# Filter spectra stored twice in DRAM, the last filter unit dealt out over two stages, the last convolution block loaded ahead

## The chip, the cores and the metric

The kernel runs on one core of one Trainium2 chip. The metric is device time in microseconds (us): the median of three runs. A core has TensorE (PE, matrix products into PSUM), VectorE (DVE), ScalarE (ACT), GpSimd (POOL) and SyncE (SP). Sixteen DMA engines move data between DRAM and on-chip memory (SBUF, 128 partitions); here SyncE's queue issues nearly all transfers. Each queue is worked off in order: an issue that waits holds up everything behind it.

## The reference

One layer on 2048 positions of 1024 channels, in float32:

```
p   = rmsnorm(x) @ w_in                      # 512 Fourier channels, 3 x 512 Hyena
y_f = rmsnorm(Re(FFT2 of the Fourier channels in 8 groups of 64))
x1, x2, v = split(short_conv(p[:, 512:]))    # three taps
k   = filters(...)                           # 2 orders x 512 channels x 4096 taps, unit norm
z   = x1 * (long_conv(v, k[0]) + d[0] * v)   # FFT over 4096 points
z   = x2 * (long_conv(z, k[1]) + d[1] * z)
y_h = rmsnorm(z)
x   = x + concat(y_f, y_h) @ w_out
out = rmsnorm_final(x + relu(rmsnorm(x) @ w_fc1)**2 @ w_fc2)
```

The filters come from a small sine network on positions, times a decay, and are normalised; `long_d` holds the d.

## The kernel before

Products that need it are made of three passes over split high and low parts. In order of time: the projection (`project`, until 410 us), with a generator `tables` run between its steps that loads tables; the Fourier mix (`fourier`) together with the first filter units, until about 475; the other filter units until 628; the long convolutions (`hyena`) until about 855; the output projection and the two MLP products until the end.

**Filters** (`filters`, lines 496 to 652). Eight units, one for each order n (0, 1) and each tile ct of 128 channels. `generate(q)`, q = 0 to 7, makes an eighth of a filter: four products into PSUM (L529), times the decay read from DRAM (`dec`, two buffers, one for two q), split into `kh` and `kl`, squares summed on GpSimd. `normalise` turns the sum into a scale and folds `long_d` in; `skip` puts it on the first tap. `stage1(c)` is the first step of a 4096-point transform, turned by VectorE (L443, tile `Gk`); `stage2(q)` is the second, with the table `f2` as the stationary operand (L597), copied to `ks` by ScalarE (L600) and stored by SyncE for two q together (L602) into the scratch `kd` ("spec" in the profile). A spectrum lies there as 128 rows: 64 frequencies of the real part, then 64 of the imaginary part.

While unit i goes through its sixteen steps (eight of `stage1`, eight of `stage2`), unit i + 2 is generated between them, by the list GENERATE; unit 7 is generated within unit 5's steps. Within unit 6's second half unit 7's `stage1` runs too (LAST). When tile `zz` is free (it held a unit's filter), v is read back into it (L648) and scaled by the product of the two filters' scales (`scale`, L582). A planner sets the order on each queue from program order and its own cost model, and moves instructions ahead where an engine would be idle.

**Convolutions** (`hyena`, from L655). Eight blocks, one for each (n, ct). `first(c)` and `second(q)` transform the input (L691, L698), with the same `f2`; `spectrum(q)` reads an eighth of the spectrum; y = pz * ks[:, 0] + (swapped, signed pz) * ks[:, 1], the first product on VectorE, the second on GpSimd, the sum on either (L704 to L706). `inverse(q)` (L714), `turn(c)` and `gate(q)` go back and multiply with the gate, read as `xg` (L670). Steps of up to four blocks are interleaved; the inverse is three steps behind (LAG). For the multiplication every partition needs both the real and the imaginary part, so `spectrum` reads the rows twice, by two transfers of 64 partitions into a tile with four buffers:

```
ks = hp.tile([P, 2, 4, 128], F32, tag="ks", name="ks", bufs=4)
src = kd[...][:, 4 * q : 4 * q + 4, :].rearrange("(s p) f c -> p s f c", s=2)
for hf in (slice(0, 64), slice(64, 128)):
    nc.sync.dma_start(ks[hf], src)
```

After the last block's steps come its gates and inverse, `Out.ahead` (the Fourier rows of the first two tokens' tiles are read, normalised, turned and multiplied with the first half of `w_out`), and `Out.weights`, which reads `w_out` and splits it into the tiles G and V that the blocks used.

Of the kernel before, what the change touches and what calls it, by code (L numbers as in the profile page):

```python
# [10 lines left out]
F32 = mybir.dt.float32  # L11
# [15 lines left out]
def _tables():  # L27
# [3 lines left out]
    T = {}  # L31
# [52 lines left out]
    A2[:, 0, 0] *= 0.5  # L84
    T["f2"] = F2.reshape(128, 32, 128).astype(f32)
# [49 lines left out]
def hybrid_block(ctx: ExitStack, tc: tile.TileContext, A, out):  # L135
# [9 lines left out]
    kd = [[scratch(f"spec{i}{n}", [P, 32, 128]) for n in range(2)] for i in range(4)]  # L145
# [350 lines left out]
    def filters(ctx, fp, gp, zp, zzs, norms, emb, wo, e1k, f2):  # L496
# [6 lines left out]
        rows = fp.tile([8, 128], F32, tag="dk8", name="dk8")  # L503
        for n in range(2):
            nc.sync.dma_start(rows[4 * n : 4 * n + 4, :], A["long_d"].rearrange("a (c n) j -> n (a c) j", n=2)[n])
        p = pa("plongd")
        nc.tensor.transpose(p[:, 0:8], rows, ident[0:8, 0:8])
        nc.scalar.copy(longd, p[:, 0:8])

        class Unit:  # L510
# [83 lines left out]
            def stage2(self, q):  # L594
# [6 lines left out]
                if q % 2:  # L601
                    nc.sync.dma_start(kd[self.ct][self.n][:, 4 * q - 4 : 4 * q + 4, :], self.ks)  # L602
# [12 lines left out]
        GENERATE = [(3, 5, 7, 7, 9, 11, 13, 15)] * 5 + [(7, 7, 8, 9, 10, 11, 12, 13)]  # L615

        LAST = ((), (), (), (), (), (0, 1, 2), (3, 4, 5), (6, 7))
        for i, u in enumerate(units):
            new = units[i + 1] if i < 7 else None

            def generate(step):
                for q in range(8 if i < 6 else 0):
                    if GENERATE[i][q] == step:
                        units[i + 2].generate(q)

            for c in range(8 if new else 0):
                u.stage1(c)
                if i == 0 and c == 6:
                    new.normalise()
                generate(c)  # L630
            for q in range(8):
                u.stage2(q)
                if i == 6:
                    for c in LAST[q]:
                        new.stage1(c)
                if i and new and q == (0 if i == 6 else 1):
                    new.normalise()

                if new and q == (2, 5, 5, 5, 5, 5, 4)[i]:
                    new.skip()  # L640
                generate(8 + q)
                if q % 4 == 0 and i > 4:
                    ct = 2 * i - 11 + q // 4
                    if 0 <= ct < 4:
                        cs = slice(128 * ct, 128 * ct + 128)
                        if ct == 0:
                            zzs.append(zp.tile([P, NT, 512], F32, tag="zz", name="zz"))
                        nc.sync.dma_start(zzs[0][:, :, cs], gd[0][:, :, cs])  # L648
                j = 8 * i + q - 50
                if 0 <= j < 8:  # L650
                    units[j // 2].scale(2 * (j % 2), nc.gpsimd)
                    units[j // 2].scale(2 * (j % 2) + 1, nc.vector)


    def hyena(hp, wp, rp, zz, e1, b1, f2, a2, out_weights, out_ahead):  # L655
# [6 lines left out]
        class Block:  # L662
            def __init__(self, n, ct):
                self.n, self.ct = n, ct
                self.cs = slice(128 * ct, 128 * ct + 128)
                self.y, self.ahead = {}, None
# [5 lines left out]
            def spectrum(self, q):  # L672

                ks = hp.tile([P, 2, 4, 128], F32, tag="ks", name="ks", bufs=4)
                src = kd[self.ct][self.n][:, 4 * q : 4 * q + 4, :].rearrange("(s p) f c -> p s f c", s=2)
                for hf in (slice(0, 64), slice(64, 128)):
                    nc.sync.dma_start(ks[hf], src)
# [16 lines left out]
            def second(self, q):  # L694
                ks = self.ahead if q == 0 and self.ahead else self.spectrum(q)
# [10 lines left out]
                (nc.gpsimd if self is not blocks[7] and q in (0, 1, 2, 3) else nc.vector).tensor_add(y, y, zs)  # L706
# [32 lines left out]
        for i in range(8):  # L739
            cur, old, older, new = (blocks[j] if 0 <= j < 8 else None for j in (i, i - 1, i - 2, i + 1))  # L740
            for q in range(8):
                if new and q == 7:
                    new.ahead = new.spectrum(0)
# [12 lines left out]
                if old and q == 3:  # L756
                    old.load()
                if new:
# [3 lines left out]
        old.load()  # L762
        for q in range(8 - LAG, 8):
            old.inverse(q)
        ahead = out_ahead(hp)
# [667 lines left out]
```

## Time and profile before

| | us |
|---|---|
| median of 3 runs | 2326.68 (2323.57 to 2328.45) |
| the profiled execution | 2326.34 |
| its span in the profile | 2324.5 |
| TensorE busy | 2244.5 (97%) |
| VectorE busy | 1514.7 (65%) |
| ScalarE busy | 1108.8 (48%) |
| GpSimd busy | 827.4 (36%) |

The profile is of one execution. A row of a group gives line, engine, operation, output <- inputs by the program's names, shapes, count, then busy time and the mean of one in ns, then idle time before them and what ended it. "SPq" and "ACTq" are the queues that issue transfers. In a timeline the columns are start, duration, engine, line, operation; in square brackets the idle time before it and its releaser. "PEclk" is the granted TensorE clock (1.00 is full). The rows themselves stand in the prediction.

### The profile page before, as it was taken

How to read it: one execution, taken by the hardware profiler on the slowest of the kernel's cores; microseconds unless marked ns; L12 is line 12 of the kernel's file. 1: busy time of each engine (PE TensorE's matmuls, PEld its weight loads, DVE VectorE, ACT ScalarE, POOL GpSimd, SP SyncE). 2: the span in 40 equal slices, each digit the busy share in tenths (PEclk: the TensorE clock that was granted, in tenths of full speed). 3: DMA queues.
4: the chain of work that ended last, by engine and by line, in shares of the span. 5: the costliest groups of instructions: out<-in, count | busy, mean ns of one | idle time of the engine just before them, and what ended most of it. 6: DMA issues, size and time to landing. Idle time of an engine off the chain costs nothing.

```text
span 2324.5 us, 31068 instructions
## 1 busy us (share of the span) xinstructions
PE 2244.5 (97%) x11025; PEld 1859.5 (80%) x11025; DVE 1514.7 (65%) x2256; ACT 1108.8 (48%) x1842; POOL 827.4 (36%) x625
## 2 busy tenths in 40 slices
PE   7999999899999979998999999999999999999998
PEld 6887788698888758886788877888888888888886
DVE  6999676677677775457544456444366666866667
ACT  6555211465455554445555556555543333533334
POOL 3444332567366532116655556555400000000000
PEclk9999999999999999999999999999999999999999
DMA  7535986557689985667544455444479766866631
GB/s 253 182 136 197 330 303 244 189 194 240 223 194 204 206 235 163 186 177 233 162 152 153 151 205 193 150 150 150 160 283 361 241 191 193 291 207 191 198 119 73
DMA packets 294716, 468.42 MB, mean 202 GB/s; under 512 B 18389, under 2 KB 142623, under 8 KB 290209
## 3 DMA queue, kind: packets, MB, share of 16 engines
q1 hardware_dynamic: 288897, 452.04, 61.3%
q10 hardware_dynamic: 5664, 14.41, 1.8%
q8 instruction: 86, 1.41, 0.3%
q14 instruction: 69, 0.57, 0.1%
HBM read 312.54 MB, written 152.27 MB: 200 GB/s over the span
## 4 chain that ended last, share of the span: by engine, by line
PE 62%; DMA 4%; DVE 4%; ACT 2%; issue 1%; POOL 1%; SPq 1%; POOLq 0%; DVEq 0%; ACTq 0%
PE p1u L189 5%; PE p1u L191 5%; PE p1u L190 5%; PE p2u L191 5%; PE p2u L189 5%; PE p2u L190 5%; PE p2v L189 3%; PE p2v L191 2%; PE p2v L190 2%; PE p1v L189 2%; PE p1v L191 2%; PE p1v L190 2%; DMA ks<-spec 2%; PE po L190 2%; PE po L191 2%; PE po L189 2%
## 5 line engine op out<-in xcount | busy, mean ns | idle before, releaser
L181 ACT CAST qahm<-ra 128x1024 fp32r<-128x1024 f32 x110 | 115.9, 1053 | 345.8 <-PE p2u L190 172.7
L182 DVE TENSOR_TENSOR qalm<-ra,qahm 128x1024 fp32r<-128x1024 f32 x110 | 134.6, 1224 | 154.6 <-ACT qahm L181 151.8
L1208 POOL TENSOR_TENSOR acc<-acc,gfin 128x512 f32<-128x512 f32 x4 | 5.1, 1277 | 633.0 <-DMA out<-acc 625.8
L189 PE MATMUL pu<-wh,xh 128*128 128x512 f32 x512 | 204.2, 400 | 5.8 <-ACT wh L184 4.6
L190 PE MATMUL pu<-wl,xh 128*128 128x512 f32 x512 | 201.1, 393 | 3.3 <-DVE wl L185 3.3
L191 PE MATMUL pu<-wh,xl 128*128 128x512 f32 x512 | 200.9, 393 | 1.7 <-DVE xl L182 1.6
L190 PE MATMUL p2u<-qblm,qahm 128*128 128x512 f32 x504 | 196.2, 389 | 0.5 <-DVE qblm L182 0.5
L189 PE MATMUL p2u<-qbhm,qahm 128*128 128x512 f32 x504 | 196.0, 389 | 0.0
L191 PE MATMUL p2u<-qbhm,qalm 128*128 128x512 f32 x504 | 195.8, 389 | 0.0
L182 DVE TENSOR_TENSOR qblm<-rb,qbhm 128x1024 fp32r<-128x1024 f32 x110 | 134.0, 1218 | 1.9 <-ACT qbhm L181 1.9
L380 POOL TENSOR_TENSOR acc<-acc,cw 128x512 f32<-128x512 f32 x45 | 59.4, 1320 | 201.5 <-DVE acc L357 200.0
L181 ACT CAST ahm<-s 128x512 fp32r<-128x512 f32 x124 | 76.6, 620 | 95.2 <-PE p1v L190 54.6
L182 POOL TENSOR_TENSOR alm<-W,ahm 128x512 fp32r<-128x512 f32 x63 | 85.3, 1354 | 92.9 <-ACT ahm L181 92.9
L189 PEld LDWEIGHTS pu<-wh,xh 128*128 128x128 f32 x512 | 97.1, 190 | 26.4 <-ACT wh L184 5.0
L181 ACT CAST qbhm<-rb 128x1024 fp32r<-128x1024 f32 x110 | 115.4, 1049 | 5.2 <-DMA a1m<-c 3.4
L190 PEld LDWEIGHTS pu<-wl,xh 128*128 128x128 f32 x512 | 97.1, 190 | 24.2 <-DVE wl L185 3.8
L191 PEld LDWEIGHTS pu<-wh,xl 128*128 128x128 f32 x512 | 97.0, 189 | 23.1 <-DVE xl L182 2.5
L190 PEld LDWEIGHTS p2u<-qblm,qahm 128*128 128x128 f32 x504 | 94.6, 188 | 20.6 <-DVE qblm L182 1.0
L189 PEld LDWEIGHTS p2u<-qbhm,qahm 128*128 128x128 f32 x504 | 94.5, 188 | 20.2 <-ACT qbhm L181 0.4
L191 PEld LDWEIGHTS p2u<-qbhm,qalm 128*128 128x128 f32 x504 | 94.6, 188 | 19.8
L189 PE MATMUL p1u<-bm,ahm 128*128 128x512 f32 x252 | 100.2, 398 | 7.2 <-ACT ku L1071 6.3
L181 ACT CAST ahm<-W 128x512 fp32r<-128x512 f32 x94 | 57.6, 615 | 102.5 <-PE p1u L190 96.0
(387 smaller groups left out, 6449.2 us busy)
## 6 DMA issues: line engine op xcount, KB each, us to landing
W<-in_w_fc SPq DMA_DIRECT2D x66, 512.0 KB, 4.6
ks<-spec SPq DMA_DIRECT2D x128, 256.0 KB, 6.6
rb<-td SPq DMA_DIRECT2D x64, 512.0 KB, 4.2
ra<-a1m SPq DMA_DIRECT2D x56, 512.0 KB, 6.8
ra<-a0m SPq DMA_DIRECT2D x54, 512.0 KB, 10.6
rb<-in_w_fc SPq DMA_DIRECT2D x46, 512.0 KB, 4.5
f<-in_w_fc SPq DMA_DIRECT2D x16, 1024.0 KB, 6.8
td<-f SPq DMA_DIRECT2D x16, 1024.0 KB, 5.2
```

Source lines behind the costliest of these rows:

```text
L181: nc.scalar.copy(hi, src)
L182: (eng or nc.vector).tensor_sub(lo, src, hi)
L189: nc.tensor.matmul(o, lhsT=lh, rhs=rh, start=start, stop=False, skip_group_check=more)
L190: nc.tensor.matmul(o, lhsT=lh, rhs=rl, start=False, stop=False, skip_group_check=more)
L191: nc.tensor.matmul(o, lhsT=ll, rhs=rh, start=False, stop=stop, skip_group_check=more)
L380: nc.gpsimd.tensor_add(m1, m1, cw[:, 3, :])
L1208: nc.gpsimd.tensor_mul(acc[i][:, c], acc[i][:, c], gfin[:, c])
```

## The change

The spectrum is written twice and read with one transfer of 128 partitions: the scratch gets the shape (copy, frequency, part, rest), the two parts of a frequency side by side. For that `stage2` gives its rows in the order frequency, part; a second table `f2k` with its columns in that order is loaded in place of `f2`, and while the last unit's `stage2` is done with an eighth after another, `f2` is loaded over it. The store is issued by ScalarE and reads its source twice. The read of `long_d` moves from `filters` to `tables`. Unit 7 is generated in unit 5's second and unit 6's first half; the reads and scalings of `zz` and the steps of the last stage are listed anew. The last block reads its spectra 2 to 7 at its second step, 4 to 7 of them into a tile of the pool `raws`; its gates, the Fourier rows and the first four parts of `w_out` are read within its steps; the work after it is ordered anew, and the tiles that take `w_out` and later the MLP's input alternate between G and V.

```diff
+    T["f2k"] = np.ascontiguousarray(F2.transpose(0, 1, 2, 4, 3)).reshape(128, 32, 128).astype(f32)
...
-    kd = [[scratch(f"spec{i}{n}", [P, 32, 128]) for n in range(2)] for i in range(4)]
+    kd = [[scratch(f"spec{i}{n}", [2, 64, 2, 32 * 128]) for n in range(2)] for i in range(4)]
...
-        rows = fp.tile([8, 128], F32, tag="dk8", name="dk8")
-        for n in range(2):
-            nc.sync.dma_start(rows[4 * n : 4 * n + 4, :], A["long_d"].rearrange("a (c n) j -> n (a c) j", n=2)[n])
...
                 if q % 2:
-                    nc.sync.dma_start(kd[self.ct][self.n][:, 4 * q - 4 : 4 * q + 4, :], self.ks)
+                    dst = kd[self.ct][self.n].rearrange("h p s x -> (p s) h x")[:, :, 512 * q - 512 : 512 * q + 512]
+                    nc.scalar.dma_start(dst, self.ks.rearrange("p (h f) c -> p h (f c)", h=1).broadcast_to([P, 2, 1024]))
+                    if self is units[7]:
+                        nc.sync.dma_start(f2[:, 4 * q - 4 : 4 * q + 4], A["f2"][:, 4 * q - 4 : 4 * q + 4])
...
-        GENERATE = [(3, 5, 7, 7, 9, 11, 13, 15)] * 5 + [(7, 7, 8, 9, 10, 11, 12, 13)]
-        LAST = ((), (), (), (), (), (0, 1, 2), (3, 4, 5), (6, 7))
+        GENERATE = {(i, step): (i + 2, q) for i in range(5) for q, step in enumerate((3, 5, 7, 8, 9, 11, 13, 15))}
+        GENERATE.update({(5 + at // 16, at % 16): (7, q) for q, at in enumerate((7, 9, 11, 13, 15, 17, 19, 21))})
+        LOAD = {(4, 8): 0, (4, 12): 1, (5, 8): 2, (5, 12): 3}
+        SCALE = {(4, 13): 0, (4, 15): 1, (5, 1): 2, (5, 4): 3, (6, 1): 4, (6, 4): 5, (7, 8): 6, (7, 9): 7}
+        LAST = ((), (), (), (), (), (0, 1), (2, 3, 4), (5, 6, 7))
...
-                ks = hp.tile([P, 2, 4, 128], F32, tag="ks", name="ks", bufs=4)
-                src = kd[self.ct][self.n][:, 4 * q : 4 * q + 4, :].rearrange("(s p) f c -> p s f c", s=2)
-                for hf in (slice(0, 64), slice(64, 128)):
-                    nc.sync.dma_start(ks[hf], src)
+                if self is blocks[7] and q > 3:
+                    if q == 4:
+                        self.room = rp.tile([P, 4, 2, 4, 128], F32, tag="W", name="ks4")
+                    ks = self.room[:, q - 4]
+                else:
+                    ks = hp.tile([P, 2, 4, 128], F32, tag="ks", name="ks", bufs=4)
+                src = kd[self.ct][self.n].rearrange("h p s x -> (h p) s x")[:, :, 512 * q : 512 * q + 512]
+                nc.sync.dma_start(ks.rearrange("p s f c -> p s (f c)"), src)
...
-                (nc.gpsimd if self is not blocks[7] and q in (0, 1, 2, 3) else nc.vector).tensor_add(y, y, zs)
+                (nc.gpsimd if q in ((0, 1) if self is blocks[7] else (0, 1, 2, 3)) else nc.vector).tensor_add(y, y, zs)
...
+                if i == 7:
+                    if q == 1:
+                        cur.ahead.update((k, cur.spectrum(k)) for k in range(2, 8))
+                    elif q == 5:
+                        ahead = work.ahead(hp)
+                        next(ahead)
+                        for k in range(4):
+                            work.load(hp, k)
+                    elif q == 6:
+                        cur.load()
...
-        ahead = out_ahead(hp)
-        next(ahead)
+        for k in range(0, 2):
+            work.weights(hp, k)
         for q in range(4):
             older.gate(q)
-            old.turn(2 * q)
-            old.turn(2 * q + 1)
-        next(ahead, None)
-        for k in range(0, 4):
-            out_weights(hp, k)
-        for q in range(4):
+        for k in range(2, 4):
+            work.weights(hp, k)
+        next(ahead)
+        for c in range(8):
+            old.turn(c)
+        for q in (0, 2):
+            next(ahead)
             old.gate(q)
-        next(ahead, None)
+            old.gate(q + 1)
         for k in range(4, 8):
-            out_weights(hp, k)
+            work.weights(hp, k)
...
-                n = "G" if k < 4 else "V"
+                n = "GVGV"[k // 2]
...
-                nc.sync.dma_start(f2[:, f : f + 8], A["f2"][:, f : f + 8])
+                nc.sync.dma_start(f2[:, f : f + 8], A["f2k"][:, f : f + 8])
```

More of the change, by code (lines that the diff above doesn't have):

```diff
@@ L493, in fourier, with filters @@
             yield
-    def filters(ctx, fp, gp, zp, zzs, norms, emb, wo, e1k, f2):
+    def filters(ctx, fp, gp, zp, zzs, norms, emb, wo, e1k, f2, dk8):
         e1h, e1l = (fp.tile([P, P], FR, tag=n, name=n) for n in ("e1h", "e1l"))
@@ L502, in filters @@
         longd = fp.tile([P, 8], F32, tag="longd", name="longd")
-        rows = fp.tile([8, 128], F32, tag="dk8", name="dk8")
-        for n in range(2):
-            nc.sync.dma_start(rows[4 * n : 4 * n + 4, :], A["long_d"].rearrange("a (c n) j -> n (a c) j", n=2)[n])
         p = pa("plongd")
-        nc.tensor.transpose(p[:, 0:8], rows, ident[0:8, 0:8])
+        nc.tensor.transpose(p[:, 0:8], dk8, ident[0:8, 0:8])
         nc.scalar.copy(longd, p[:, 0:8])
@@ L629, in filters @@
                     new.normalise()
-                generate(c)
+                others(c)
             for q in range(8):
                 u.stage2(q)
+                if new and q == (2, 5, 5, 5, 5, 5, 5)[i]:
+                    new.skip()
                 if i == 6:
@@ L635, in filters, with hyena @@
                         new.stage1(c)
-                if i and new and q == (0 if i == 6 else 1):
+                if i and new and q == (2 if i == 6 else 1):
                     new.normalise()
[L639 to L655, printed above, removed]
+                others(8 + q)
+    def hyena(hp, wp, rp, zz, e1, b1, f2, a2, work):
         def big(nm):
@@ L665, in __init__ @@
                 self.cs = slice(128 * ct, 128 * ct + 128)
-                self.y, self.ahead = {}, None
+                self.y, self.ahead = {}, {}
             def load(self):
@@ L694, in second @@
             def second(self, q):
-                ks = self.ahead if q == 0 and self.ahead else self.spectrum(q)
+                ks = self.ahead.pop(q) if q in self.ahead else self.spectrum(q)
                 p = pa("pz2")
@@ L742, in hyena @@
                 if new and q == 7:
-                    new.ahead = new.spectrum(0)
+                    new.ahead[0] = new.spectrum(0)
                 cur.second(q)
@@ L1316, in tables @@
             got.append(load(cpool, "gy", [P, 8], A["g_y"]))
+            got.append(cpool.tile([8, 128], F32, tag="dk8", name="dk8"))
+            for n in range(2):
+                nc.sync.dma_start(got[-1][4 * n : 4 * n + 4, :], A["long_d"].rearrange("a (c n) j -> n (a c) j", n=2)[n])
             f2, emb = (pl.tile([P, 32, P], F32, tag=n, name=n) for pl, n in ((tp, "f2"), (ep, "emb")))
@@ L1350, in hybrid_block @@
         spx = early.enter_context(ExitStack())
-        filt = filters(spx, fp, gp, zp, zzs, norms, emb, wo, e1k, f2)
+        filt = filters(spx, fp, gp, zp, zzs, norms, emb, wo, e1k, f2, dk8)
         with pool("fourier", "right") as fo:
@@ L1367, in hybrid_block @@
             with pool("hyena") as hp:
-                hyena(hp, wp, rp, zz, e1z, b1, f2, a2, work.weights, work.ahead)
+                hyena(hp, wp, rp, zz, e1z, b1, f2, a2, work)
             tabs.close()
```

33 lines of the change are left out of this document (23 added, 10 removed).

## The prediction

> **What bounds the kernel now.** I read the page's first part, then the stretches the change touches one by one (stages of the program, not equal slices), then TensorE's waits in them. The columns of the first view are the stretch, its length, busy time of each engine with instructions, granted clock, DMA share and GB/s.
>
> ```profile
> PE 2244.5 (97%) x11025; PEld 1859.5 (80%) x11025; DVE 1514.7 (65%) x2256; ACT 1108.8 (48%) x1842; POOL 827.4 (36%) x625
> ```
> ```profile
> 410.00:418.60 8.60, 0.17 (x1) 0.00 (x0) 5.18 (x8) 0.00 (x0) 3.74 (x3) 0.68 0.81 272
> 418.60:423.00 4.40, 4.36 (x12) 3.06 (x13) 0.91 (x2) 1.29 (x5) 0.00 (x0) 0.50 0.72 253
> 423.00:441.00 18.00, 18.00 (x84) 11.45 (x83) 16.17 (x25) 7.69 (x13) 11.09 (x9) 0.99 0.30 89
> ...
> 476.00:556.00 80.00, 80.00 (x602) 73.36 (x601) 57.82 (x103) 50.54 (x101) 57.65 (x50) 1.00 0.60 204
> 556.00:592.00 36.00, 34.26 (x271) 31.49 (x270) 28.69 (x52) 22.97 (x48) 28.57 (x22) 1.00 0.96 291
> 592.00:602.50 10.50, 6.68 (x34) 5.24 (x32) 10.47 (x15) 3.48 (x6) 8.05 (x7) 0.92 0.89 309
> 602.50:607.70 5.20, 5.17 (x24) 5.17 (x25) 1.35 (x7) 1.27 (x3) 0.00 (x0) 0.50 0.00 0
> 607.70:628.00 20.30, 19.49 (x142) 17.41 (x142) 8.03 (x11) 8.94 (x17) 3.50 (x2) 1.00 0.44 174
> ...
> 643.00:806.00 163.00, 158.45 (x1119) 138.09 (x1118) 125.01 (x195) 93.97 (x163) 101.52 (x89) 1.00 0.89 201
> 806.00:862.00 56.00, 43.50 (x247) 30.66 (x248) 42.85 (x70) 30.77 (x50) 14.62 (x14) 0.91 0.86 223
> ```
> ```profile
> PE pv L714 <- DVE y L706: 13.0, 15, 3.0
> PE plongd L507 <- DMA dk<-in_long_d: 8.5, 1, 8.5
> PE pk L597 <- DVE Gk L443: 6.1, 3, 3.8
> ```
>
> TensorE sets the time; what can be won is its idle time between 410 and 862 and the time it runs at half clock after an idle stretch. From 476 to 556, where filters are generated, it is busy 80.00 of 80 us: there is nothing to win, only to lose. The holes are one of 8.5 us at 410, 3.82 at 592 (10.50 less 6.68), 4.55 spread over 643 to 806, and 12.5 in 806 to 862, the end of the long convolution. The last two have DMA shares of 0.89 and 0.86 at 201 and 223 GB/s, while 476 to 556 moves 204 GB/s with a share of only 0.60.
>
> **Part 1, long_d read early.** SyncE issues that read behind the last gate stores, and the first decay read behind it:
>
> ```profile
> 416.51 0.61 SPq L505 DMA_DIRECT2D dk<-in_long_d  x2
> 417.24 0.35 SPq L170 DMA_DIRECT2D dec<-in_decay  x1
> ...
> 421.48 0.69 DVE L533 TENSOR_TENSOR kt<-pk,dec 128x512 f32<-128x512 f32 x1 [4.89 <-DMA dec<-in_decay]
> ```
>
> Read during the projection, it leaves this place: the 8.5 us go. What is late next is the decay read: it moves up by 417.24 - 416.51 = 0.73 us, so VectorE gets it at 420.75. Until then TensorE can fill its eight PSUM banks and stops. From there VectorE is the limit: its work up to 441 is 0.91 + 16.17 = 17.1 us, which ends at 437.8 instead of 441. I take -3.2. Bounds: -0.7 (all hangs on the decay read) and -10.7 (8.5 plus half of the 4.36 us run at clock 0.50). The granted clock is 0.68 in 410 to 418.6 and 0.50 until 423. If it halves in the new stop as well (about 416 to 421), the eight filled banks cover it: five turns and three products, 5 x 0.69 + 3 x 0.69 = 5.5 us of VectorE, while the clock recovered 4.4 us after the start at 418.6. So -3.2 stands with either clock. The Trainium skill, TensorE: Matmul & The Clock Gate, Part 1, has the clock halve after an idle window of about 3.4 us; by that rule it halves again in the new stop, and the sum is the same.
>
> **Part 2, stores twice, from ScalarE.** The 32 stores of 512 KB become 32 of 1 MB; the issue leaves SyncE for ScalarE, whose own issues take 0.33 us:
>
> ```profile
> 371.97 0.33 ACTq L348 DMA_DIRECT2D xc<-xt  x1
> ```
> ```profile
> spec<-ks SPq DMA_DIRECT2D x31, 512.0 KB, 2.6
> dec<-in_decay SPq DMA_DIRECT2D x27, 512.0 KB, 4.2
> zz<-gates SPq DMA_DIRECT2D x4, 1024.0 KB, 7.9
> ```
>
> 32 x 0.33 = 10.6 us of ScalarE, which is busy 50.54 of 80 there: about 2 more per 25, beside TensorE's work, 0. The bytes: 476 to 556 spends 0.60 x 80 = 48 us of DMA time on 204 GB/s x 80 us = 16.3 MB, so 2.9 us per MB, 1.5 per 512 KB. Sixteen more halves there are 24 us: the share goes from 0.60 to 0.91. It fits, and the decay reads that share the engines land later than 4.2.
>
> ```profile
> 616.94 0.89 PE pk L597 x8
> ```
>
> Such a read is issued when step 8 of a unit frees its buffer and used at step 13; five parts of a second stage at 0.89 us (eight matmuls, the row above) and two or three generations of the same eight make a lead of about 6.7 us. I take 0; bounds 0 and +24 (the rival below). SyncE's shorter queue wins nothing, since TensorE waits for none of its transfers there.
>
> **Part 3, the last unit spread, gates fetched and scaled earlier.** From 592 VectorE is the limit: 10.47 of 10.5 us busy while TensorE waits 3.82, and then runs 5.17 us at half clock (2.6 lost). The same multiplications, splits and transposes are only dealt out anew:
>
> ```profile
> 593.62 0.40 PE L189 MATMUL pk<-kh,e1h 128*128 128x512 f32 x1
> ...
> 594.32 0.39 PE L189 MATMUL pk<-kh,e1h 128*128 128x512 f32 x1
> ```
> ```profile
> L443 DVE STREAM_TRANSPOSE Gk<-pk 128x512 f32<-128x512 f32 x16 | 10.5, 692 | 0.9 <-PE pk L191 0.9
> L582 DVE TENSOR_TENSOR zz<-zz,norms 128x512 f32<-128x512 f32 x4 | 5.1, 1324 | 0.1
> L182 DVE TENSOR_TENSOR kl<-kt,kh 128x512 fp32r<-128x512 f32 x2 | 1.8, 898 | 0.0
> L533 DVE TENSOR_TENSOR kt<-pk,dec 128x512 f32<-128x512 f32 x2 | 1.3, 676 | 0.0
> ```
>
> A first-stage part takes TensorE 0.70 us (594.32 - 593.62). In unit 6's first stage VectorE now has 8 x 0.69 + 3 x (0.68 + 0.90) + 2 x 1.32 = 12.9 us against TensorE's 8 x 0.70 + 3 x 0.89 = 8.3, so the hole stays at about 4 us and perhaps halves the clock as before; what gets better is 556 to 592 (1.74 idle). The sum of squares of the last unit is also needed sooner after its last part. I take -1; bounds -8 (1.74 + 3.82 + 2.6) and +4.
>
> **Part 4, the f2 table in two orders.** Four loads of 512 KB into the table while the last unit's second stage drains it: 6 us of DMA time beside 4 MB of stores (12 us), from about 622. The block's first stage keeps TensorE busy for 7 us after 628 without the table or a spectrum, and the first inverse comes at 643. The backlog of some 15 us is through by 637 or 638. I take +0.5; bounds 0 and +5, what it costs if that cover is gone.
>
> **Part 5, spectra by 128 partitions.**
>
> ```profile
> ks<-spec SPq DMA_DIRECT2D x116, 256.0 KB, 6.6
> ```
> ```profile
> W<-in_w_fc SPq DMA_DIRECT2D x30, 512.0 KB, 4.6
> ```
>
> Two 256 KB halves of 64 partitions land in 6.6 us each; 512 KB over 128 partitions land in 4.6. The halves also cost two SyncE issues of 0.6 us:
>
> ```profile
> L677 SPq DMA_DIRECT2D ks<-spec x128: 573/605/4396, 628.6 to 828.1; - x128
> ```
>
> One transfer is thus there 2 us sooner. The DMA share of 0.89 is 24 us of a block's 27; the gate read has up to 9 of them, the 2.1 MB of spectra at least 15; at part 2's 2.9 us per MB these take 6, so the share falls to about 15 of 27, 0.55. TensorE's waits for y end with a late ks on GpSimd:
>
> ```profile
> 817.57 10.51 DMA xg<-gates
> 828.09 8.03 DMA ks<-spec
> ...
> 836.28 1.46 POOL zs L705
> ...
> 838.60 1.14 PE pv L714 x8
> ```
>
> Between 643 and 806 at most 4.55 us of idle time go; some of it hangs on VectorE's order of transposes, so -3.5 (bounds 0 and -4.5).
>
> **Part 6, the last block loaded ahead.** Here the chain above stands: a gate read of 10.5 us and behind it a spectrum read of 8.0. With all six last spectra asked for at its second step, in part into other room, the y waits that lie here, at least 13.0 - 4.55 = 8.45 us, mostly go. Then the end:
>
> ```profile
> 839.66 3.66 PE L727 MATMUL pb<-G,b 128*64 128x512 f32 x16
> 846.67 1.11 PE L810 MATMUL pt_y<-ident,yf 128*128 128x128 f32 x4 [3.35 <-ACT yf L827]
> ...
> 849.36 5.66 PE L727 MATMUL pb<-W,b 128*64 128x512 f32 x16
> ```
>
> The Fourier rows come ahead, and one token's first product stands between the turns and the last gates, so the wait of 3.35 us for yf and what the 5.66 us have over the same sixteen matmuls' 3.66 (2.0, the half clock) can go. That is up to 8.45 + 3.35 + 2.0 = 13.8. Against it:
>
> ```profile
> L704 DVE TENSOR_TENSOR y<-pz,ks 128x512 f32<-128x512 f32 x51 | 33.7, 670 | 5.9 <-DMA ks<-spec 3.0 <-ACT zs L702 2.2 <-ACT V L715 0.3
> ...
> L443 DVE STREAM_TRANSPOSE W<-V 128x512 f32<-128x512 f32 x48 | 30.6, 676 | 6.4 <-ACT V L715 6.3
> ```
>
> In the last block's steps 3 to 7 VectorE has two y operations a step and eight turns (10 x 0.67 + 8 x 0.68 = 12.1 us) for TensorE's ten groups of eight (8.9 us), so some 3 us stay, and the eight turns after the last inverse (5.4) are only partly covered. I take -9; bounds 0 and -13.8.
>
> **Sum.** -3.2 + 0 - 1 + 0.5 - 3.5 - 9 = -16.2. The profiled execution took 2326.3 us (span 2324.5), 0.3 below the median of 2326.7, so no correction: 2310.
>
> **Rivals.** *The limit moves* (VectorE and GpSimd set the pace where the spectra did): the idle time of parts 5 and 6 keeps another releaser and halves to -6; with -3 for the rest, 2317. For it: VectorE is busy 42.85 of 56 in the last stretch; against it: the longest waits of the chain are transfers.
>
> *More than forecast*: VectorE turns Fourier tiles while it waits, the clock stays up at 592 and in the end: -8, -5, -4 and -12, with the table's +0.5, gives 2298. For it: each of these holes has clock 0.50 behind it.
>
> *Slower: decay reads behind doubled stores.* With a share of 0.91 (and 0.96 already from 556 to 592, where gate reads and doubled stores meet) a decay read waits for a 1 MB store, 3.1 us of DMA time, once its landing passes the lead of 6.7 us. Two reads a unit fall into the storing half; at 2 us each over six units that is +24, and with the gains elsewhere 2334. For it: TensorE has no slack at all there. Against it: 4.2 + 3.1 = 7.3 is just past the lead, and eight PSUM banks lie between. It decides from about 7 us to landing. The Trainium skill, DMA: Bandwidth & Descriptors, Issuing engines are not separate DMA queues, says that issues from different engines share the same 16 DMA engines and that a second queue saves only issue time; by that rule the ScalarE queue gives the stores no room of their own.
>
> *The reads were hidden*: the 64-partition form was no cost, and parts 5 and 6 win only what loading earlier brings, -5: 2317 to 2318, inside the first rival's case.
>
> **How the numbers follow.** Forecast (2303 to 2315) 0.50; limit moves 0.21, a fifth of that above 2322; more than forecast 0.13; slower rival 0.16, of which 0.10 ends past 2331 and 0.06 within the bound, where it eats the gain. A difference under 0.2% (4.7 us: 2322.0 to 2331.3) can't be told from none. So faster 0.50 + 0.17 + 0.13 = 0.80, same 0.04 + 0.06 = 0.10, slower 0.10. Range: 2296 to 2326, which holds the middle of the case above the forecast, all of the first rival's and the unknown costs of parts 3 and 4, and leaves out the slower case's 0.10 and a little below; the forecast's own is 2303 to 2315.
>
> **What would show it.** Right: no plongd wait and VectorE idle for the decay read near 416 to 421; the DMA share from the second block to the seventh near 0.55 with spectra landing in 5 us or less; 806 to 862 shorter by about 9. Wrong: waits of kt for dec in 476 to 600, idle TensorE there; first spectrum later than 640; a stretch after 628 in which TensorE still waits for y though ks has landed.

## The result, and the profile after

The changed kernel takes 2337.7 us (2335.6 to 2339.3) where the kernel before takes 2326.7 (2321.7 to 2328.5): the ratio is 1.0051, with an interval of 1.0036 to 1.0066. 2310 was forecast, with a range of 2296 to 2326. The profiled execution has a span of 2334.6 us, 10.1 more than before. From its page, the busy times of the engines:

```profile
PE 2244.7 (96%) x11025; PEld 1858.4 (80%) x11025; DVE 1505.8 (64%) x2254; ACT 1110.1 (48%) x1842; POOL 832.1 (36%) x627
```

TensorE's busy time is the one of before (2244.5) to 0.2 us. The 10 us are waits. To find where they lie, I cut both executions at the same pieces of work: the last Fourier product, the last filter product, the first block's last inverse, the last block's last inverse, the last output product. The stretches of before and after (columns as in the prediction):

```profile
464.20:627.50 163.30, 156.87 (x1139) 142.72 (x1139) 116.98 (x211) 92.71 (x191) 104.72 (x87) 0.98 0.65 216
627.50:663.50 36.00, 34.74 (x233) 32.16 (x232) 23.21 (x34) 18.33 (x32) 20.00 (x19) 1.00 0.80 197
663.50:839.70 176.20, 163.49 (x1146) 139.82 (x1144) 134.49 (x211) 97.42 (x168) 101.69 (x89) 0.99 0.92 207
839.70:1060.90 221.20, 214.61 (x1041) 173.63 (x1040) 123.95 (x343) 110.25 (x252) 47.68 (x36) 0.98 0.63 189
```
```profile
459.70:640.30 180.60, 160.55 (x1140) 144.02 (x1139) 111.17 (x209) 91.63 (x187) 102.57 (x86) 0.97 0.79 277
640.30:686.60 46.30, 37.07 (x233) 33.56 (x233) 23.89 (x44) 21.21 (x40) 20.10 (x20) 0.93 0.94 311
686.60:849.40 162.80, 159.78 (x1147) 138.48 (x1147) 135.44 (x211) 102.19 (x172) 105.41 (x91) 0.99 0.72 217
849.40:1070.10 220.70, 213.56 (x1040) 173.24 (x1040) 121.43 (x332) 104.03 (x241) 48.72 (x36) 0.98 0.59 180
```

| stage | before | after | difference |
|---|---|---|---|
| until the last Fourier product | 464.2 | 459.7 | -4.5 |
| filters | 163.3 | 180.6 | +17.3 |
| first convolution block | 36.0 | 46.3 | +10.3 |
| blocks 2 to 8 | 176.2 | 162.8 | -13.4 |
| gates, turns, output projection | 221.2 | 220.7 | -0.5 |
| the rest of the span | 1263.6 | 1264.5 | +0.9 |

So the gains came: 18.4 us, where parts 1, 5 and 6 took 15.7. But the filters and the first block lost 27.6 us, where parts 2 to 4 together took a gain of 0.5. The gains first: one spectrum lands in 4.0 us (before, each half of one took 6.6), and from 690 to 812, in the blocks behind the first, TensorE has no idle time left.

```profile
ks<-spec SPq DMA_DIRECT2D x45, 512.0 KB, 4.0
```
```profile
690.00:812.00 122.00, 122.00 (x859) 104.53 (x858) 99.73 (x156) 70.97 (x122) 76.98 (x69) 1.00 0.71 212
```

The losses, as TensorE's waits in the filters and in the first block:

```profile
PE pdk L569 <- DVE both L562: 6.5, 2, 5.5
PE pk L597 <- DVE Gk L446: 4.8, 4, 2.1
PE psum_k L553 <- POOL acc L547: 3.8, 1, 3.8
PE pdk L569 <- DVE dk L558: 2.6, 2, 1.6
...
PE pv L726 <- DVE v_f L219: 4.3, 1, 4.3
PE pz L710 <- DVE G L446: 3.9, 2, 3.0
```

Before, `Gk` was the only wait of more than 0.3 us in the filters. New are `pdk` and `psum_k`: TensorE stands at the product that `skip` or `normalise` needs, and the small steps of the normalisation are late. No wait for a decay read is among them, nor in VectorE's list for this stage. The longest, from the timeline:

```profile
563.83 0.69 DVE L582 TENSOR_TENSOR zz<-zz,norms 128x512 f32<-128x512 f32 x1 [1.28 <-DMA zz<-gates]
563.94 3.39 POOL L582 TENSOR_TENSOR zz<-zz,norms 128x512 f32<-128x512 f32 x2 [1.49 <-DMA zz<-gates]
...
569.03 0.63 ACT L543 ACTIVATE sqr<-kt 128x512 f32<-128x512 f32 x1 [4.93 <-POOL acc L544]
...
569.57 0.19 ACT L200 ACTIVATE sq_k<-vk 128x1 f32<-128x1 f32 x1
...
572.48 0.20 DVE L562 TENSOR_SCALAR both<-nw_k 128x1 f32<-128x1 f32 x1
...
572.71 0.58 PE L569 MATMUL pdk<-ident,dk 128*1 128x128 f32 x2 [5.49 <-DVE both L562]
```

GpSimd scales v for 3.39 us ahead of the running sum; ScalarE's next square waits 4.93 us for that sum; the square root of the normalisation (`sq_k`) stands behind the square in ScalarE's queue; TensorE waits 5.49 us. The clock follows:

```profile
567.20:571.00 3.80, 0.02 (x1) 0.00 (x0) 2.01 (x4) 1.23 (x3) 3.80 (x4) 0.99 0.87 300
571.00:577.70 6.70, 4.99 (x22) 4.16 (x23) 2.27 (x8) 5.05 (x12) 5.21 (x5) 0.50 0.96 283
```

The clock halves 3.8 us into the idle time and stays at half for 6.7 us. The Trainium skill, TensorE: Matmul & The Clock Gate, Part 1, has this after an idle window of about 3.4 us; the trace agrees.

In the first block it is one transfer that ScalarE waits for:

```profile
659.30 0.60 SPq L677 DMA_DIRECT2D xg<-gates  x1
...
664.17 0.61 SPq L828 DMA_DIRECT2D yf<-yfd  x1
...
671.44 1.16 PE L710 MATMUL pz<-G,f 128*128 128x128 f32 x8 [3.05 <-DVE G L446]
674.71 0.29 ACT L692 COPY ks<-ks 1x128 f32<-1x128 f32 x1 [9.70 <-DMA ks<-spec]
...
676.90 2.05 PE L726 MATMUL pv<-y,a 128*128 128x128 f32 x8 [4.30 <-DVE v_f L219]
```

`spectrum(0)` of the second block has a copy of one row (L692) in ScalarE's queue. It waits 9.70 us for its read, and all of ScalarE's work behind it with it. In front of that read stand the table, the doubled stores of the last unit, two gate reads and, from 664, Fourier rows that are used only after the last block. The kernel before reads these rows at 830; the planner has moved them up.

### The profile page after: what moved, and what is told of

It is laid out like the page before. It is cut to its first block, busy times and chain, and to the rows that moved or that the text cites. A ratio compares the mean times of both kernels' runs of the same rounds, so it can differ in the third digit from the quotient of the medians.

```text
span 2334.6 us, 30973 instructions
## 1 busy us (share of the span) xinstructions
PE 2244.7 (96%) x11025; PEld 1858.4 (80%) x11025; DVE 1505.8 (64%) x2254; ACT 1110.1 (48%) x1842; POOL 832.1 (36%) x627
## 4 chain that ended last, share of the span: by engine, by line
PE 49%; DVE 2%; DMA 1%; issue 1%; ACT 1%; POOL 0%; SPq 0%; DVEq 0%; ACTq 0%; POOLq 0%
PE p2u L193 5%; PE p2u L192 5%; PE p2u L194 5%; PE p1u L194 5%; PE p1u L192 5%; PE p1u L193 5%; PE p2v L192 2%; PE p2v L194 2%; PE p2v L193 2%; PE p1v L192 2%; PE p1v L194 2%; PE p1v L193 2%; PE p2m L192 1%; PE p2m L193 1%; PE p2m L194 1%; PE p1m L192 1%
## 6 DMA issues: line engine op xcount, KB each, us to landing
ra<-a0m SPq DMA_DIRECT2D x54, 512.0 KB, 10.6
```

## The experiments

Each run had runs of the kernel before beside it; ratios go to these. "Filters" and "first block" are the stages of the table above, from each run's own trace. There is one trace for each kernel, and a stage that an edit leaves alone is not always as long. The rest of the span, behind the output projection, takes 1261.5 to 1265.0 us in these traces, and the gates, turns and output projection of before 219.3 to 221.6; 2 or 3 us in one such long stage of one trace show nothing. The first block of before is steadier: 35.3 to 36.0 us in eight traces (41.5 in b_twice_sp).

| run | median us | ratio (interval) | filters | first block |
|---|---|---|---|---|
| before | 2326.7 | 1 | 163.3 | 36.0 |
| the change | 2337.7 | 1.0051 (1.0036 to 1.0066) | 180.6 | 46.3 |
| a_oldloop | 2336.5 | 1.0053 (1.0036 to 1.0071) | 182.9 | 47.3 |
| b_twice | 2341.5 | 1.0071 (1.0043 to 1.0099) | 183.3 | 35.4 |
| a_nof2 | 2332.5 | 1.0024 (1.0010 to 1.0038) | 182.6 | 41.8 |
| a_oldtail | 2334.3 | 1.0031 (1.0014 to 1.0049) | 180.8 | 46.1 |
| b_twice_sp | 2354.6 | 1.0110 (1.0083 to 1.0137) | 183.7 | 41.5 |
| a_spstore | 2354.1 | 1.0109 (1.0087 to 1.0131) | 198.7 | 47.3 |
| a_oldloop_sp | 2342.4 | 1.0066 (1.0041 to 1.0090) | 186.3 | 47.3 |
| a_sp_yf | 2354.9 | 1.0115 (1.0094 to 1.0137) | 197.2 | 43.5 |
| b_act | 2323.3 | 0.9980 (0.9968 to 0.9992) | 163.0 | 35.4 |
| b_twice_hp_acc | 2347.6 | 1.0087 (1.0060 to 1.0114) | 185.0 | 35.4 |
| a_hp_acc | 2355.1 | 1.0118 (1.0093 to 1.0144) | 197.1 | 46.7 |
| a_hp_acc_yf | 2359.5 | 1.0137 (1.0109 to 1.0164) | 196.7 | 45.7 |
| b_twice_ord | 2333.1 | 1.0016 (1.0004 to 1.0028) | 168.4 | 35.3 |
| b_act_late | 2341.6 | 1.0059 (1.0044 to 1.0074) | 178.5 | 35.3 |
| a_ord | 2326.9 | 0.9997 (0.9984 to 1.0011) | 171.2 | 46.4 |
| a_yf_ord | 2330.5 | 1.0016 (1.0005 to 1.0028) | 171.7 | 44.0 |
| best1 | 2319.5 | 0.9969 (0.9956 to 0.9982) | 162.3 | 35.3 |
| best2 | 2317.0 | 0.9961 (0.9946 to 0.9975) | 161.6 | 35.3 |

**Which part costs what.** My first theory was the new filter loop, since the stall at 567 shows v being scaled in front of a sum. a_oldloop puts the old loop back into the changed kernel (the two main lists; the code around them goes back too):

```diff
-        GENERATE = {(i, step): (i + 2, q) for i in range(5) ...
-        SCALE = {(4, 13): 0, ...
+        GENERATE = [(3, 5, 7, 7, 9, 11, 13, 15)] * 5 + [(7, 7, 8, 9, 10, 11, 12, 13)]
```

> The changed kernel with the filter loop of before put back (the lists of generation, of the last stage and of the gate reads and scalings, and the places of normalise and skip); the doubled stores from ScalarE, the second table, the spectra by 128 partitions and the work at the end stay as changed. Theory 'loop': the 17 us lost between the end of the Fourier mix and the end of the filters (180.6 us after, 163.3 before) come from the new order, in which the scalings and the later fourth generation stand ahead of the normalisation's small steps on GpSimd, VectorE and ScalarE. Then this stage falls to 163 to 167 us and the time to 2320 to 2325. Rival 'stores': ScalarE's 32 store issues and the doubled bytes hold up the squares and casts; then the stage stays at 176 us or more and the time within 4 us of 2338. Either way the stall of 3.05 and 4.30 us after the first block's first products stays.

The filters took 182.9 us: no gain, and the theory fell. The planner set the scalings ahead of the sums there too, and TensorE waits 5.80 us at the same product. b_twice takes only the doubled stores into the kernel before:

```diff
-    nc.sync.dma_start(kd[self.ct][self.n][:, 4 * q - 4 : 4 * q + 4, :], self.ks)
+    dst = kd2[self.ct][self.n].rearrange("h p f c -> p h (f c)")[:, :, 512 * q - 512 : 512 * q + 512]
+    nc.scalar.dma_start(dst, self.ks.rearrange("p (h f) c -> p h (f c)", h=1).broadcast_to([P, 2, 1024]))
```

> The kernel before with one edit: each spectrum store goes to two copies in DRAM and is issued by ScalarE; the reads take the first copy, as before. Theory 'loop': the filter stage stays at 163 to 165 us, since TensorE waits for none of this; only behind the last unit 2 MB more stand ahead of the first spectra, at the 2.5 us per MB that 400 GB/s give about 5 us, of which 7 us of the first block's first stage hide most: 2327 to 2331. Rival 'stores': most of the 17 us come here too: 2338 to 2345.

The rival was right: 183.3 us. With the loop of before, doubled stores from ScalarE lose 20.0 us in the filters, and nothing in the first block (35.4).

a_nof2 leaves the second load of f2 out (L605 to L607), so that the convolutions use the table in the wrong order:

> The changed kernel without the second load of the table f2 during the last unit's second stage; the long convolutions then use the table in the filters' order, so their values are others. Theory 'backlog': between 640 and 655 the DMA engines are full at about 400 GB/s, and the 2 MB of the table stand ahead of the first spectra; without them the first spectrum lands about 5 us sooner (653 becomes 648), the wait of 0.89 goes and the stall of 7.35 us near 670 shrinks or goes together with the half clock behind it: time 2337.7 less 6 to 11, so 2327 to 2332. Rival 'early reads': the gate read of the second block and the Fourier rows, issued from 659 on, make the stall near 670 by themselves; then only 1 to 3 us go: 2335 to 2337.

The first block shortened from 46.3 to 41.8 us: 4.5 are the table's. The rest of the loss, 5.8 us, stays; both theories hold a part.

a_oldtail puts back the last block and the end as they were:

> The changed kernel with the last block's loading and the work behind it as before (spectra one by one, gate read, Fourier rows and w_out behind the last step, the order of gates, turns and products of before). Theory 'part 6 gains early and gives back nothing late': the last block's waits for y come back, its last inverse is 5 to 8 us later than 849.4, the work behind it stays within 2 us of 220.7: 2342 to 2346. Rival 'no gain': with spectra by 128 partitions the waits for y do not come back, and the new order of the end costs as much as it saves: 2336 to 2339.

Its last two stages show blocks 2 to 8 as long without part 6 as with it (162.8), and the work behind them 2.9 us shorter than the 220.7 of the change:

```profile
689.00:852.20 163.20, 159.47 (x1146) 138.24 (x1145) 136.48 (x213) 101.07 (x171) 102.41 (x89) 0.99 0.72 217
852.20:1070.00 217.80, 213.16 (x1041) 172.36 (x1040) 120.78 (x332) 105.13 (x242) 47.76 (x36) 0.98 0.61 182
```

The rival 'no gain' was right, and more: what part 6 was to win was won by part 5 already. As a whole the run is 3.4 us shorter than the change, but the intervals of the two ratios overlap, so what the new end costs is not shown. And although the program has the end of before again, the Fourier rows are still read in the first block:

```profile
666.93 0.62 SPq L807 DMA_DIRECT2D yf<-yfd  x1
```

The same holds for every kernel here that reads the spectra by 128 partitions and gives the rows their own buffers; in every kernel that reads them by 64 they come at 826 or later.

**Queue or bytes.** Doubling the bytes and moving them to ScalarE came together. The same stores from SyncE:

```diff
-    nc.scalar.dma_start(dst, ...
+    nc.sync.dma_start(dst, ...
```

> The kernel before with its stores doubled (second copy not read) and issued by SyncE as before. Doubled stores from ScalarE lost 20.1 us in the filter stage (183.3 us against 163.3). Theory 'queue': not the bytes but the queue does it; on ScalarE the stores stand among the squares and the square root that normalise needs, and SyncE, rid of them, asks for v earlier, so that the scalings come ahead of the sums. Then the stage is within 3 us of 163.3 here and the time 2327 to 2331 (2 MB more ahead of the first spectra). Rival 'bytes': landing and buffers do it; then the stage stays at 178 us or more and the time above 2338.

> The changed kernel with its doubled stores issued by SyncE instead of ScalarE, nothing else. Theory 'queue': the filter stage falls from 180.6 us to 163 to 168; the stall near the first block's end (7.35 us and the half clock) stays, since the table and the last stores still stand ahead of the first spectra: 2321 to 2326. Rival 'loop': the new order of generating and scaling is at fault too: stage above 174, time 2332 to 2338. Rival 'bytes': no change, 2336 to 2340.

> The changed kernel with the filter loop of before and stores from SyncE; the doubled stores, the two tables, the spectra by 128 partitions and the work at the end stay. Theory 'queue': the stage is 163 to 167 us, as before, and the time 2321 to 2326; against the run that differs only by the loop it shows what the new loop is worth once the queue is put right: within 3 us. Rival 'loop': the new loop loses 10 us or more against this one. Rival 'bytes': both stay at 2336.

'Queue' fell in all three: from SyncE the doubled stores lose as much or more. In b_twice_sp the decay reads stand behind the stores in SyncE's queue and land later than the 4.2 us of before:

```profile
dec<-in_decay SPq DMA_DIRECT2D x23, 512.0 KB, 6.0
```

VectorE still waits for them only 1.3 us in all, so this is not what loses the 20 us there.

With these stores the new loop does lose against the old one, 198.7 against 186.3 us. The groups of waits of a_spstore show TensorE waiting for the sums of the last two units, 16.4 us in two waits (6.0 and 10.4):

```profile
PE psum_k L553 <- POOL acc L547: 16.4, 2, 10.4
```

a_sp_yf is a_spstore with the two early Fourier rows put where they can't be read early:

```diff
-            y = self.fourier_rows(t, hp, "yf", 2)
+            y = self.fourier_rows(t, hp, "zs", 4)
```

> The changed kernel with stores from SyncE, and the two Fourier rows that the last block prepares put into buffers of zs instead of their own, so that they can only be read once the last block has used those buffers and not, as now, near 664 in the first block. Theory 'early reads': they and their root mean square on ScalarE and VectorE take part in the stall near 670; 3 to 6 us less than the same kernel without this edit. Rival 'backlog': the table, the last stores and the gates alone fill the DMA engines until 675; 0 to 1 us less. Rival 'the end pays': read late, they hold up the first products after the last block: the same or 1 to 3 us more.

The first block went from 47.3 to 43.5 us, so the rows cost 3.8 there. The time did not fall: blocks 2 to 8 take 1.6 us longer and the gates, turns and output projection 2.6 ('the end pays').

**Order or bytes.** b_act moves the stores of before to ScalarE and leaves them single:

```diff
-    nc.sync.dma_start(kd[self.ct][self.n][:, 4 * q - 4 : 4 * q + 4, :], self.ks)
+    nc.scalar.dma_start(kd[self.ct][self.n][:, 4 * q - 4 : 4 * q + 4, :], self.ks)
```

> The kernel before with its single stores issued by ScalarE, nothing else. In the program VectorE's order in units 3 to 6 is then the one of before (four turns, a decay product, a turn, a decay product, two turns, two decay products, then the normalisation with one product inside); with doubled stores the planner puts the decay products behind more turns (from ScalarE: four turns, a product, three turns, two products, and three products inside the normalisation; from SyncE: all eight turns first). Theory 'order': it is this order, which the planner derives from larger stores, that makes the sums and the normalisation late; with single stores the filter stage is within 2 us of 163.3 and the time 2325 to 2330. Rival 'queue': ScalarE's issues cost by themselves: stage 170 us or more, 2333 or more.

```profile
464.40:627.40 163.00, 156.34 (x1139) 142.16 (x1139) 113.68 (x209) 92.29 (x188) 104.43 (x87) 0.99 0.67 220
```

That is its filter stage, 163.0 us: ScalarE's queue costs nothing. It is the size of the stores. But size has two effects. The one is more bytes. The other shows when the traces of b_act and b_twice are laid side by side: with doubled stores the planner writes another order. From 440 us on, 64 of VectorE's 1733 instructions and 19 of ScalarE's 1618 stand elsewhere, and a few of the other engines'. To set the order against the bytes I first gave squares, sums and normalisation priority in the planner (shown for the squares and sums; the normalisation gets the same):

```diff
+                    with tc.high_priority(offset=300):
                         nc.scalar.square(sq, k4)
                         nc.gpsimd.tensor_add(self.acc, self.acc, sq)
```

> The kernel before with doubled stores from ScalarE (2341.5 us), and with the squares, their sums and the normalisation given priority in the planner. Bytes, queue and TensorE's order are the same as in that run; VectorE's order in units 4 to 6 goes back to four turns, a decay product, a turn, a decay product, with the normalisation's steps right behind the sum. Theory 'order': the filter stage falls from 183.3 to 164 to 170 us and the time to 2327 to 2333; unit 4 keeps some of its 9 us, as v is still scaled there. Rival 'bytes': the decay reads and the stores of 8 us landing hold it; then the stage stays above 178 us and the time above 2337.

> The changed kernel with the same priority for squares, sums and normalisation, nothing else. Theory 'order': the filter stage falls from 180.6 to 164 to 171 us, the stall near 670 stays: 2321 to 2329. Rival 'bytes': 176 or more, 2333 to 2338.

These two runs do not separate the theories. The priority put the squares in front of the cast with which `skip` ends, and TensorE now waited for that (the groups of waits of b_twice_hp_acc; L577 is the cast there):

```profile
PE pk L190 <- ACT kh L577: 11.3, 4, 5.4
```

So they say nothing on order against bytes, and neither does the same with late Fourier rows:

> The same as the run before this one, and the last block's Fourier rows in buffers of zs, so that they are read late. With the stores from SyncE this edit shortened the way from the last filter product to the first block's last inverse by 3.8 us and lost 0 to 1 of it at the end. Theory 'early reads': 2 to 4 us less than the run without it: 2318 to 2326. Rival 'nothing': within 1 us of it.

It took 2359.5 us; its filters lost as much. The first block is 1.0 us shorter than in the run without late rows (46.7 to 45.7).

The clean exchange: b_act and b_twice have the same instructions and differ in the size of 32 stores. In each I wrote the engines' orders of the other in as dependencies, one chain per engine (shortened):

```diff
         hybrid_block(tc, A, out)
+        for names in order.values():
+            row = [named[n] for n in names]
+            for first, then in zip(row, row[1:]):
+                tc.add_manual_dep(then, first.name, NoSync)
```

> The kernel before with doubled stores from ScalarE, and every engine's order written out as it stands in the same kernel with single stores from ScalarE (filter stage 163.0 us); the two programs have the same instructions and differ in the size of 32 stores alone. Theory 'order': what lost the time is the order that the planner makes of larger stores, not their landing; the stage is 163 to 167 us and the time 2326 to 2332. Rival 'bytes': the 24 MB more in the DMA engines hold up decay reads and buffers; the stage stays at 178 us or more, 2337 to 2345.

> The converse: single stores from ScalarE, with every engine's order written out as the planner made it for doubled stores. Theory 'order': the stage is 178 us or more and the time 2335 to 2343. Rival 'bytes': 163 to 166 us, 2321 to 2327.

In the traces every engine's instructions then stand in the order of the other program. (The doubled stores move 16 MB more, 32 times 512 KB, not the 24 of the first of these two expectations.) The filter stage of b_act_late (small stores in the order for large ones), and that of b_twice_ord (large stores in the order for small ones):

```profile
465.70:644.20 178.50, 160.44 (x1139) 144.45 (x1139) 115.03 (x211) 92.80 (x189) 104.65 (x88) 0.96 0.61 201
```
```profile
466.20:634.60 168.40, 158.45 (x1140) 143.37 (x1139) 113.65 (x209) 91.99 (x187) 104.88 (x87) 0.97 0.85 299
```

From 163.0 us the order alone adds 15.5, the bytes alone 5.4, both together 20.3 (183.3). The times go the same way: the ratios are 0.9980 with neither change, 1.0016 with the bytes alone, 1.0059 with the order alone, 1.0071 with both. 'Order' holds for three quarters. No run writes a program's own order into it, so what the chains cost by themselves is not shown; it can hardly be more than the 5.4 us of b_twice_ord, which has them too, and that would leave 10.1 us for the order. The bytes' share is for the most part in one place of b_twice_ord, a decay read behind doubled stores and gate reads: VectorE waits 9.27 us, and TensorE 4.6 for VectorE's product.

```profile
593.14 0.69 DVE L534 TENSOR_TENSOR kt<-pk,dec 128x512 f32<-128x512 f32 x1 [9.27 <-DMA dec<-in_decay]
```
```profile
PE pk L530 <- DVE kt L534: 4.6, 1, 4.6
```

How the order loses is seen in b_act and b_act_late at the same place, VectorE in one unit. In b_act two turns stand between the first and the second decay product of the unit, and one product between the sum (vk) and the reciprocal (the expectation left out one turn):

```profile
510.78 0.65 DVE L533 TENSOR_TENSOR kt<-pk,dec 128x512 f32<-128x512 f32 x1
511.36 0.69 DVE L443 STREAM_TRANSPOSE Gk<-pk 128x512 f32<-128x512 f32 x1
...
512.12 0.70 DVE L443 STREAM_TRANSPOSE Gk<-pk 128x512 f32<-128x512 f32 x1
512.75 0.64 DVE L533 TENSOR_TENSOR kt<-pk,dec 128x512 f32<-128x512 f32 x1
```

In b_act_late four turns stand there, and three products between the sum and the reciprocal:

```profile
514.50 0.69 DVE L533 TENSOR_TENSOR kt<-pk,dec 128x512 f32<-128x512 f32 x1 [0.20 <-DVE kl L182]
515.11 0.71 DVE L443 STREAM_TRANSPOSE Gk<-pk 128x512 f32<-128x512 f32 x1
...
515.84 1.95 DVE L443 STREAM_TRANSPOSE Gk<-pk 128x512 f32<-128x512 f32 x3
517.72 0.65 DVE L533 TENSOR_TENSOR kt<-pk,dec 128x512 f32<-128x512 f32 x1
```

TensorE's wait there, from the groups of waits of b_act_late:

```profile
PE pdk L569 <- DVE dk L558: 9.5, 4, 5.6
```

The second product comes 3.22 us after the first (517.72 - 514.50) instead of 1.97, the sums and the normalisation with it, and TensorE, whose own order is nearly the same in both, waits at `pdk` (2.3 us in b_act). Whether VectorE's order alone does it, without ScalarE's, was not tried.

The same exchange in the changed kernel, with the orders that the planner makes if it is shown single stores:

> The changed kernel with every engine's order written out as the planner makes it if it is shown the changed kernel with single stores. Bytes, queues and instructions are those of the changed kernel. Theory 'order': the filter stage falls from 180.6 to 163 to 168 us; the stall near the end of the first block (7.35 us and half clock) stays; 2320 to 2327. Rival 'bytes': 176 us or more, 2334 to 2340.

> The same with the last block's Fourier rows in buffers of zs, so that they are read in the last blocks and not near 664. Theory 'early reads': 2 to 4 us less than the run without this edit, as the way from the last filter product to the first block's last inverse shortened by 3.8 us with stores from SyncE. Rival 'nothing': within 1 us, since the second block's gate and the table still fill the DMA engines.

The filters fell from 180.6 to 171.2 us and the time to 2326.9: with the good order the changed kernel is as fast as the one before, and no faster. 171.2 lies between the two theories. In the changed kernel the order is thus 9.4 of the 17.3 us that the filters lost; 7.9 stay. What is left are waits for the turns, 12.3 us where it was 6.1 before, and two waits of VectorE for decay reads:

```profile
PE pk L597 <- DVE Gk L446: 12.3, 7, 5.9
```
```profile
DVE kt L533 <- DMA dec<-in_decay: 4.7, 2, 2.8
```

The bytes, 5.4 us in the kernel before, can hold most of the 7.9; this was not taken apart in the changed kernel. The first block stays at 46.4. The late Fourier rows shortened it by 2.4 us, and the last block (3.9) and the work behind it (1.6) lost more.

**A faster version.** best1 is the kernel before with long_d read early and single stores from ScalarE; best2 adds the last block's loading ahead, by 64-partition transfers and with the old order of the end:

> The kernel before with two edits: long_d read during the projection, as in the change, and the single stores issued by ScalarE. The first moved the end of the Fourier mix from 464.2 to 459.7 in the changed kernel; the second by itself gave a ratio of 0.998. Theory: both add up, since the filter stage keeps its order with single stores: 4 us less than 2323.3, so 2317 to 2321, faster than both kernels. Rival: the filter stage gives the 4.5 us back, because the earlier start changes the planner's order: 2322 to 2326.

> The same, and the last block's spectra 2 to 7 read at its second step (4 to 7 into the other room) and its gate read within its steps, as in the change, still by transfers of 64 partitions and with the order of the end as before. Theory 'ahead': the waits of the last block's y for a late spectrum behind the gate read go, about 5 us of them, and nothing is lost at the end: 2 to 6 us less than the run before this one, 2312 to 2318. Rival 'hidden': the 64-partition reads still fill the DMA engines, VectorE's turns take the place of the waits: within 1.5 us of it.

Both beat both kernels: 0.9969 (0.9956 to 0.9982) and 0.9961 (0.9946 to 0.9975). In best1 the 3.4 us of the early start are still there after the filters (4.3 against b_act), but the convolutions of its trace end where those of b_act do (837.5 and 837.3), and the intervals of the two ratios overlap: that the early read adds to b_act's gain is not shown. What best2 adds is inside the intervals; its trace has 17.2 us from the seventh block's last inverse to the eighth's, against 21.5 in best1.

## Why the prediction was wrong, by its own steps

**Part 1** was right: no wait of `plongd`, and VectorE waits for the decay read, at 421.27 where 420.75 was forecast; -4.5 us where -3.2 was taken. The seven traces with `long_d` read late end the Fourier mix at 463.8 to 467.0, 465.5 in the mean, the thirteen with the early read at 459.6 to 463.2, 460.9 in the mean: 4.6 us. TensorE's new stop was 2.94 us long, not about 5, and the clock did not halve in it (1.00 from 413 to 424).

```profile
421.27 1.29 DVE L533 TENSOR_TENSOR kt<-pk,dec 128x512 f32<-128x512 f32 x2 [3.93 <-DMA dec<-in_decay]
```

**Part 2 is the step that failed.** The filters lost 17.3 us where this term was taken at 0. "It fits", "I take 0" counted ScalarE's 10.6 us, the DMA share and the lead of the decay reads, and took the order of VectorE, ScalarE and GpSimd as given. The share did rise (0.65 to 0.79 over the stage), the queue did cost nothing, and the bytes cost 5.4 us in the kernel before. But a planner made the order and makes it anew when a transfer has another size: 15.5 us in the kernel before, 9.4 in the changed one. What is left of the 17.3 there, 7.9, is not taken apart, and why the planner's model sets the turns ahead stays open.

**The slower rival** had the sign and the place, and nearly the size (+24; the filters lost 17.3), but another mechanism. It wanted decay reads past 6.7 us and waits of kt for dec: in the changed kernel they land in 4.3 us, and there is no such wait. What it describes happened once in b_twice_ord (9.27 us) and twice in a_ord (4.7 us together).

**Part 3** did not bring its -1 in a way that shows: the changed kernel against a_oldloop takes 180.6 and 182.9 us, both in the planner's order. The new loop is not the cause of the 17.3 us, but with stores from SyncE it lost 12 us, outside its bound of +4. The hole of 3.8 us that it was to shorten turned up at the last unit's sum instead (`psum_k`, 3.8 us), and with the good order, in a_ord, it is 5.9 us. The sentence that this sum is needed sooner named the right place.

**Part 4 failed.** "The backlog is through by 637 or 638" gave +0.5. The filters ended 12.8 us later, and from there the DMA engines were full for 20 us:

```profile
640.30:660.00 19.70, 17.82 (x102) 15.47 (x102) 11.04 (x17) 6.68 (x12) 5.42 (x7) 1.00 1.01 388
```

The first block measured +10.3 us. The table's 4.5 us are near the upper bound of 5. What was missing altogether are the reads that the planner moves up: the second block's gate read and the Fourier rows. That it does so because SyncE has half as many spectra to issue fits the runs, but its model was not examined. The rows are worth 1.0 to 3.8 us there, by three pairs of traces; of the 10.3 us some 2 to 5 stay open. The gate read was not tried by itself.

**Part 5** was right in its mechanism and too small: -3.5 taken, bound -4.5, while blocks 2 to 8 won 13.4 us, 13.0 of them without part 6 (176.2 less 163.2; 8.9 in blocks 2 to 7 and 4.1 in the last). The waits of the last block were put down to part 6; faster spectra alone removed them. The DMA share is 0.71, not 0.55: a share of 0.71 that moves 212 GB/s is 3.3 us of DMA time per MB, against 2.9 assumed and 4.4 in the blocks of before (0.92 at 207). The Trainium skill, DMA: Bandwidth & Descriptors, Rules for kernel authors, has two transfers to the two halves of the partitions serialise and advises one of 128. The advice agrees with 256 KB in 6.6 us against 512 KB in 4.0; no run here shows the serialising by itself.

**Part 6** brought nothing that shows here (-9 taken, bound 0): the last block's waits were gone without it, and the end is 2.9 us longer with its new order than without, in one trace each. On 64-partition reads its loading ahead, in best2, shortened the last block by 4.3 us, of which 2.5 arrived in the time, less than the intervals tell.

Of the signs named beforehand, spectra in 5 us or less and the missing `plongd` wait came true; "first spectrum later than 640" and "idle TensorE in 476 to 600" came true on the wrong side.

## What to carry to other kernels

Where a planner orders the engines, a transfer's size is an input to that order: a change of bytes that the DMA engines can carry may still reorder the engine next to the critical one, so compare the orders of both programs before trusting a sum made in the old one. To tell a new order from slower data, write the order of the one program into the other, and write a program's own order into it as a control. A transfer that the planner can issue earlier may land in the one stretch that has no room for it.

## What the hardware showed that was not expected

Moving 32 single stores from SyncE to ScalarE, which leaves the filter stage as it was (163.0 us), made the kernel faster by 0.2% (0.9980, 0.9968 to 0.9992). Of the two traces, the second is 2.3 us shorter in the convolutions and 1.9 in the output projection. That is no more than such stages differ between the traces here, and the planner's order is not the same either: 31 of VectorE's 1732 instructions stand elsewhere, the last of them near 671 us. So it is not shown whether the queue, the order or something else makes the 0.2%.
